# A hybrid decoder trunk on one core: the DeltaNet inverse issued in one piece, with z projections, weight subtractions and output heads moved around it

## The chip, the cores and the metric

The kernel runs on one core of a Trainium2 chip, in float32 throughout. TensorE (PE) multiplies in a float32 form that the kernel makes exact enough by splitting each operand into a high and a low part: each product of two split operands is three matmuls. VectorE (DVE), ScalarE (ACT) and GpSimd (POOL) work beside it, and DMAs for the weights are issued from SyncE's queue (SP). The metric is the device time of one execution in microseconds; the median of several runs is compared. A difference is judged against the spread of these runs.

## The reference

Two layers over a sequence of 256 tokens, width 1024. Each layer adds half a SwiGLU, a mixer and another half SwiGLU, each on an RMS-normalised input; a final RMS norm follows. The mixer of layer 0 is a gated DeltaNet, that of layer 1 a sliding-window attention with sinks. What the change touches is the DeltaNet mixer:

```python
def mixer_gated_deltanet(h, w_in, w_conv, A_log, dt_bias, out_norm, w_out):
    proj = h @ w_in                                  # q, k, v (8 heads x 128 each), z, b, a
    qkv = jax.nn.silu(causal_depthwise_conv(qkv, w_conv))          # 4 taps
    q = l2norm(q) * 128 ** -0.5;  k = l2norm(k)
    beta = sigmoid(b);  g = -exp(A_log) * softplus(a + dt_bias)
    o = gated_delta_rule_chunked(q, k, v, g, beta)   # chunks of 64 tokens
    o = rmsnorm(o, out_norm) * jax.nn.silu(z)
    return o @ w_out
```

Inside the delta rule a unit lower triangular system (I + L) sol = rhs is solved for every head and chunk, with L from k, beta and the decay; sol gives u and w, and a scan over the chunks carries the state S. The kernel solves it by forming the inverse of I + L from small blocks upwards.

## The kernel before, in words

The input is 2 tiles of 128 tokens (t = 0, 1). Weights come in pieces of 128x1024: `split` (L287) issues a DMA into `raw` (4 buffers), ACT casts it to `whi` (L307), and an engine, DVE unless POOL is named, subtracts to get `wlo` (L308). `whi` and `wlo` have 5 buffers each. `wcols` (L319) fetches a chunk of 256 columns as two such pieces; `npool` says how many of them POOL subtracts. PSUM has four slots psA (projections) and four psB (everything else).

The order of instructions on each engine is set ahead of time: the kernel is traced in program order, which is the priority, and a planner lists the instructions by estimated readiness. `issue_after(ins)` puts the instructions of a block behind `ins` on that engine's queue. `Ticker` interleaves by hand: generators are added, and each `tick()` runs every one of them to its next `yield`.

The DeltaNet mixer (`gdn`, L672) runs as follows.

- Two chunks of z (`zproj`, L926) for both tiles, with the gates `gdn_gates` as a generator beside them. The gates end in four Exps into `Dt` (L666); `res["exp"]` is the last of them that is traced so far. A third chunk of z follows (`zmore`, L961).
- Four k chunks by `conv` (L908): two tiles of 24 matmuls each into `pcv`, a copy scaled by the fourth tap on ACT (L915, tile `cv`, pool c1 with 5 buffers), the three other taps on DVE (L918), and a Silu on ACT (L922) issued after `res["exp"]`. Behind each chunk a generator `kpost` transposes (L705), sums squares (L712), forms k k^T (L730) times the decay into `nf` (L731), and after every second chunk `blocks` cuts out the diagonal blocks and masks them on POOL (L759, L761).
- Behind the last k chunk the generator `inverse` (L766 on) inverts the 16x16 diagonal blocks of all heads on DVE, in three pieces with a `yield` between them, and starts two generators `chain`, which build the 128x128 inverses from the blocks by small matmuls on PE (L824, L844, L856, L864, L872, L878).
- Four v chunks and four q chunks by the same `conv`; `vpost` and `qpost` follow them. `state` carries the scan; `first` computes the outputs of heads 0 to 3 for t = 0 ahead of the end of the q chunks. The fourth chunk of z comes behind the third q chunk. `zgate` applies Silu to z on ACT and multiplies the output norm into it on POOL (L935).
- The end: w_out in 8 rows of 128 (`out_weights`, rows 3 and 4 subtracted on POOL), the outputs of the heads (`o_of`), their norm (`post`, L1042 to L1050), a transpose to the output's layout (`turn`, L1057 to L1061) and the output projection into `acc`, then `after(t)`, the norm for the next FFN.

The attention mixer (`swa`) fetches its w_out by the same `out_weights`, with rows 4 and 6 subtracted on POOL.

Of the kernel before, what the change touches and what calls it, by code (L numbers as in the profile page):

```python
# [24 lines left out]
H = 8  # L25
# [188 lines left out]
class Kern:  # L214
# [72 lines left out]
    def split(self, src, hi, lo, shape, eng=None, cuts=1):  # L287
        nc = self.nc
        raw = self.wp.tile(shape, F32, tag="raw", name="raw", bufs=4)
        n = shape[1] // cuts  # L290
        parts = [slice(i * n, (i + 1) * n) for i in range(cuts)]
        if len(src.shape) == 4:
            for k in range(shape[1]):
                nc.sync.dma_start(out=raw[:, k].rearrange("p (g f) -> p g f", g=2), in_=src[:, k])
        else:
            nc.sync.dma_start(out=raw, in_=src)
        with ExitStack() as behind:
            if self.hold is not None:
                self.hold[0] -= 1
                if self.hold[0] < 0:  # L300
                    for ins in self.hold[2:]:
                        behind.enter_context(self.tc.issue_after(ins.ins))
                self.hold[1] -= 1
                if not self.hold[1]:
                    self.hold = None
            for c in parts:
                nc.scalar.copy(hi[:, c], raw[:, c])  # L307
                (eng or nc.vector).tensor_tensor(out=lo[:, c], in0=raw[:, c], in1=hi[:, c].bitcast(F32), op=ALU.subtract)  # L308

    def wpiece(self, src, a, b, eng=None, pool=None):  # L310
# [5 lines left out]
        self.split(src, hi, lo, [P, a, b], eng)  # L316
        return hi, lo
# [20 lines left out]
    def wrow(self, w, k, pool=None, eng=None):  # L338
        hi, lo = self.wpiece(w[k * P:(k + 1) * P, :].unsqueeze(1), 1, D, eng=eng, pool=pool)
        return hi[:, 0, :], lo[:, 0, :]  # L340

    def wrow2(self, w, k, eng):
        hi = self.big([P, 2, 1, D], "whi2", F32R)
        lo = self.big([P, 2, 1, D], "wlo2", F32R)
        out = []
        for i in range(2):
            self.split(w[(k + i) * P:(k + i + 1) * P, :].unsqueeze(1), hi[:, i], lo[:, i], [P, 1, D], eng(k + i))
            out.append((hi[:, i, 0, :], lo[:, i, 0, :]))
        return out
# [216 lines left out]
    def gdn_prep(self, w_in, w_conv, A_log, dt_bias, out_norm):  # L566
# [13 lines left out]
        onb = self.row_bc(out_norm, P, "onb")  # L580
        wcr = self.small([96, P], "wcr", 1)
        nc.scalar.dma_start(out=wcr, in_=w_conv.rearrange("j (t c) -> (j t) c", c=P))
        return wh, wl, expA, dtb, onb, wcr
# [88 lines left out]
    def gdn(self, nrm, prep, w_in, w_out, after):  # L672
        nc = self.nc
        M = self.M
        wabh, wabl, expA, dtb, onb, wcr = prep
# [90 lines left out]
        def inverse():  # L766
# [21 lines left out]
            yield  # L788
# [13 lines left out]
            yield  # L802
# [6 lines left out]
            nc.vector.transpose(yx[:, 1].rearrange("p u c -> p (u c)"), yx[:, 0].rearrange("p u c -> p (u c)"))  # L809
# [98 lines left out]
        def conv(col0, dst, npool, start):  # L908
            w = self.wcols(w_in, col0, npool)
            for f in range(2):  # L910
# [5 lines left out]
                for j in (2, 1, 0):  # L916
                    s = 3 - j
                    nc.vector.scalar_tensor_tensor(  # L918
                        out=c[:, s:], in0=ps[:, 0:T - s], scalar=wc[:, j, ct:ct + 1],
                        in1=c[:, s:], op0=ALU.mult, op1=ALU.add)  # L920
# [11 lines left out]
        def zgate(t, hs, keep=lambda ins: ins):  # L932
            z = zs[:, t, hs]
            keep(nc.scalar.activation(z, z, AF.Silu))
            keep(nc.gpsimd.tensor_tensor(  # L935
                out=z, in0=z, in1=onb.unsqueeze(1).to_broadcast([P, hs.stop - hs.start, P]), op=ALU.mult))

        def zgates():
            n = 2 * zc[0]
            for t in range(NT):  # L940
                yield
                zgate(t, slice(0, n), self.tc.keep_in_program_order)
# [16 lines left out]
        zc = [2]  # L959

        def zmore(n):  # L961
            for c in range(zc[0], zc[0] + n):
                w = self.wcols(w_in, 3 * D + c * 256)
                for t in range(NT):
                    zproj(c, t, w)
                    tk.tick()
            zc[0] += n
# [36 lines left out]
        def state():  # L1004
# [16 lines left out]
            for g in range(2):  # L1021
                pw = four("pws", lambda o, i: mm(o, wT[:, 4 * g + i, :], S[:, 4 * g + i, :]))
                for i in range(4):
                    h = 4 * g + i
                    nc.vector.scalar_tensor_tensor(out=u[:, 1, h, :], in0=pw[:, i, :], scalar=nbr[:, 1, h:h + 1],
                                                   in1=u[:, 1, h, :], op0=ALU.mult, op1=ALU.add)
            yield
# [10 lines left out]
        def post(t, g):  # L1038
# [10 lines left out]
            for i in range(4):  # L1049
                nc.vector.scalar_tensor_tensor(out=on[:, i, :], in0=po[t, g][:, i, :], scalar=f[:, i:i + 1],  # L1050
                                               in1=zs[:, t, 4 * g + i, :], op0=ALU.mult, op1=ALU.mult)
            ons[t, g] = on

# [9 lines left out]
        def first():  # L1063
            o_of(0, 0)
            post(0, 0)
            yield
            yield
            turn(0, 0)
            yield
# [3 lines left out]
        for c in range(4):  # L1073
            conv(c * 256, lambda f: late["qT"][:, 2 * c + f, :], 1, [qpost(c)])
            if c == 0:
                tk.add(state())
            if c == 1:
                tk.add(then(first))
            if c == 2:
                n = 2 * zc[0]  # L1080
                w = self.wcols(w_in, 3 * D + 3 * 256)
                for t in range(NT):
                    zproj(3, t, w)
                    zgate(t, slice(n, H))
                    tk.tick()
# [3 lines left out]
        o_of(0, 1)  # L1089
        post(0, 1)  # L1090
        o_of(1, 0)
        acc = [self.psA("acc") for n in range(2)]
        for n in range(2):
            self.out_part(acc[n], ob[0], ws, n, range(0, 4))
        turn(0, 1)
        post(1, 0)
        o_of(1, 1)
        turn(1, 0)
        for n in range(2):
            self.out_part(acc[n], ob[0], ws, n, range(4, KT))  # L1100
            self.out_add(acc[n], 0, n)
        post(1, 1)
        turn(1, 1)
        after(0)
        for n in range(2):
            a = self.psA("acc")
            self.out_part(a, ob[1], ws, n, range(KT))
            self.out_add(a, 1, n)
# [30 lines left out]
    def swa(self, nrm, prep, w_in, w_out, after):  # L1139
# [112 lines left out]
        ws = self.out_weights(w_out, (4, 6))  # L1252
# [113 lines left out]
```

## Time and profile before

| what | before |
|---|---|
| median of 3 runs | 1028.65 us (1027.06 to 1029.8) |
| profiled execution, its own time | 1026.73 us |
| its span | 1025.0 us |
| mean granted TensorE clock | 0.996 |
| subtractions of weights in the DeltaNet stage | 31 on DVE, 12 on POOL |
| the same in the attention stage (740 to 840 us) | 21 on DVE, 2 on POOL |

In rows of the timeline the columns are the start in us, the duration in us, the engine, the line, the operation with tiles and shapes, the count, and in brackets the idle time before it with what released it. In rows of busy time by stretches the columns are the stretch, its length, then for each engine that worked (in the order PE, weight loads, DVE, ACT, POOL) the busy time with the number of instructions, and at the end the granted clock, the DMA share and GB/s; a row asked for one line has only the engines of that line. In rows of groups the busy time and the mean in ns follow the bar.

### The profile page before, as it was taken

To read this page: it belongs to the slowest core of one execution; us is meant where nothing else is said; L and a number is where in the kernel's file an instruction comes from. 1 tells how busy PE (TensorE), PEld (TensorE's weight loads), DVE (VectorE), ACT (ScalarE), POOL (GpSimd) and SP (SyncE) were. 2 spreads that over 40 slices of the span, in tenths; PEclk is the share of its full clock that TensorE was granted. 3 is DMA by queue.
4 is the path that set the end of the run, shared out by engine and by line. 5 is a ranking of instruction groups with operands and counts; after the bars stand their busy time and mean duration, and the time that the engine had idled before them with its cause. 6 is when DMAs were issued, how large, how long until landed. Compare 5 with 4: busy or idle time off the path is not lost.

```text
span 1025.0 us, 16468 instructions
## 1 busy us (share of the span) xinstructions
PE 999.7 (98%) x6195; PEld 871.3 (85%) x6195; DVE 648.1 (63%) x971; ACT 550.8 (54%) x1007; POOL 232.6 (23%) x269
## 2 busy tenths in 40 slices
PE   8999999999979899999999999999999999999997
PEld 7888888899878888888888888888898678888886
DVE  6865654666896666666546666664568756666544
ACT  6755544457755645555534555553366645555442
POOL 0124510016753201332200122230021301323100
PEclk9999999999989999999999999999999999999999
DMA  7766665644443335666665666666653436666651
GB/s 248 238 185 169 198 208 182 203 150 127 134 128 104 103 103 179 192 189 186 200 196 178 196 191 190 185 206 195 196 191 118 128 99 208 201 187 185 203 187 42
DMA packets 135316, 177.05 MB, mean 173 GB/s; under 512 B 7250, under 2 KB 120260, under 8 KB 135236
## 3 DMA queue, kind: packets, MB, share of 16 engines
q1 hardware_dynamic: 132032, 171.46, 54.6%
q10 hardware_dynamic: 3204, 4.53, 1.4%
q8 instruction: 49, 0.80, 0.3%
q14 instruction: 31, 0.25, 0.1%
HBM read 174.92 MB, written 1.05 MB: 172 GB/s over the span
## 4 chain that ended last, share of the span: by engine, by line
PE 62%; issue 1%; DVE 1%; ACT 1%; DMA 0%; POOLq 0%; POOL 0%; SPq 0%; DVEq 0%; ACTq 0%
PE pg L361 11%; PE pu L361 11%; PE acc L356 7%; PE acc L354 7%; PE acc L355 7%; PE pu L362 6%; PE pg L362 6%; PE pgu L356 1%; PE pgu L355 1%; PE pgu L354 1%; PE pq L354 1%; PE pq L356 1%; PE pq L355 1%; PE psc L1190 1%; PE po L1234 1%
## 5 line engine op out<-in xcount | busy, mean ns | idle before, releaser
L308 DVE TENSOR_TENSOR wlo<-raw,whi 128x1024 fp32r<-128x1024 f32 (+1 forms) x304 | 378.2, 1247 | 202.6 <-ACT whi L307 200.9
L307 ACT CAST whi<-raw 128x1024 fp32r<-128x1024 f32 (+1 forms) x318 | 330.1, 1046 | 186.7 <-PE acc L356 82.7
L361 PE MATMUL pg<-hs,whi 128*128 128x512 f32 x624 | 219.5, 394 | 0.0
L361 PE MATMUL pu<-hs,whi 128*128 128x512 f32 x624 | 219.4, 393 | 0.0
L362 PE MATMUL pu<-hs,wlo 128*128 128x256 f32 x624 | 175.5, 281 | 0.0
L362 PE MATMUL pg<-hs,wlo 128*128 128x256 f32 x624 | 174.6, 281 | 0.0
L361 PEld LDWEIGHTS pg<-hs,whi 128*128 128x128 f32 x624 | 117.0, 188 | 26.0
L469 POOL TENSOR_TENSOR act<-act,gate 128x256 f32<-128x256 f32 x78 | 58.6, 751 | 354.7 <-DVE act L468 345.9
L361 PEld LDWEIGHTS pu<-hs,whi 128*128 128x128 f32 x624 | 117.0, 187 | 25.9
L355 PE MATMUL acc<-wlo,ah 128*128 128x512 f32 (+1 forms) x340 | 128.5, 378 | 0.0
L356 PE MATMUL acc<-whi,al 128*128 128x512 f32 (+1 forms) x340 | 128.4, 378 | 0.0
L354 PE MATMUL acc<-whi,ah 128*128 128x512 f32 (+1 forms) x340 | 128.0, 378 | 0.0
L362 PEld LDWEIGHTS pg<-hs,wlo 128*128 128x128 f32 x624 | 118.2, 189 | 0.4
L362 PEld LDWEIGHTS pu<-hs,wlo 128*128 128x128 f32 x624 | 118.2, 189 | 0.0
L354 PEld LDWEIGHTS acc<-whi,ah 128*128 128x128 f32 x340 | 64.1, 188 | 12.1
L355 PEld LDWEIGHTS acc<-wlo,ah 128*128 128x128 f32 x340 | 64.1, 188 | 11.7
L356 PEld LDWEIGHTS acc<-whi,al 128*128 128x128 f32 x340 | 64.0, 188 | 11.8
L472 POOL TENSOR_SCALAR ah<-act 128x256 fp32r<-128x256 f32 x78 | 66.4, 851 | 6.7
L354 PE MATMUL pcv<-hs,whi 128*128 128x256 f32 x192 | 56.5, 294 | 5.9 <-DVE cv L918 5.9
L458 ACT COPY gate<-pg 128x256 f32<-128x256 f32 x78 | 28.7, 368 | 52.6 <-PE pg L362 52.6
L467 ACT COPY act<-pu 128x256 f32<-128x256 f32 x78 | 28.7, 368 | 52.0 <-PE pu L362 52.0
L356 PE MATMUL pcv<-hs,wlo 128*128 128x256 f32 x192 | 55.9, 291 | 0.0
(340 smaller groups left out, 1522.8 us busy)
## 6 DMA issues: line engine op xcount, KB each, us to landing
raw<-in_ffn_w_gu_dram SPq DMA_DIRECT2D x156, 512.0 KB, 4.5
raw<-in_ffn_w_down_dram SPq DMA_DIRECT2D x88, 512.0 KB, 4.2
raw<-in_a_w_in_dram SPq DMA_DIRECT2D x32, 512.0 KB, 4.1
raw<-in_ffn_w_gu_dram SPq DMA_DIRECT2D x40, 256.0 KB, 4.8
raw<-in_b_w_in_dram SPq DMA_DIRECT2D x12, 512.0 KB, 4.8
raw<-in_a_w_out_dram SPq DMA_DIRECT2D x8, 512.0 KB, 4.3
raw<-in_b_w_out_dram SPq DMA_DIRECT2D x8, 512.0 KB, 3.6
nw<-in_ffn_norm_dram ACTq DMA_DIRECT2D x3, 512.0 KB, 4.2
```

Source lines behind the costliest of these rows:

```text
L307: nc.scalar.copy(hi[:, c], raw[:, c])
L308: (eng or nc.vector).tensor_tensor(out=lo[:, c], in0=raw[:, c], in1=hi[:, c].bitcast(F32), op=ALU.subtract)
L354: nc.tensor.matmul(out, lhsT=lh, rhs=rh, start=start, stop=False)
L355: nc.tensor.matmul(out, lhsT=lh, rhs=rl, start=False, stop=False)
L356: return nc.tensor.matmul(out, lhsT=ll, rhs=rh, start=False, stop=stop)
L361: nc.tensor.matmul(out, lhsT=lh, rhs=r2, start=start, stop=False)
L362: return nc.tensor.matmul(out[:, :T], lhsT=ll, rhs=rh, start=False, stop=stop)
L458: nc.scalar.copy(g, pg[:, T:])
L467: nc.scalar.copy(a, pu[:, T:])
L469: nc.gpsimd.tensor_tensor(out=a, in0=a, in1=gates[f], op=ALU.mult)
L472: ahead[2] = nc.gpsimd.tensor_scalar(oh, a, 1.0, None, op0=ALU.mult)
L1190: nc.tensor.matmul(out, lhsT=qT[:, j, b * P:(b + 1) * P], rhs=kz[:, kv, :, kt * P:(kt + 1) * P], start=True, stop=True)
```

## The change

- `inverse` loses its two `yield`s, so all its steps are traced at once, and its last transpose is kept as `late["inv"]`.
- `conv` loses `npool`, and takes `behind`: the three taps on DVE of v chunks 0 and 1 are issued after `late["inv"]`. `self.hold = [0, 2, late["inv"]]` ahead of v chunk 2 does the same with the subtractions of its two weight pieces.
- z chunk 2 moves from ahead of the k convolutions to behind them; z chunk 3 moves there from the q convolutions.
- No weight subtraction is left on POOL, neither in the convolutions nor for w_out of either mixer.
- The output norm is no longer multiplied into z on POOL; it scales the rows of w_out as they are cast (ACT) and subtracted (DVE, now multiply and subtract in one instruction). It is loaded as one column.
- `heads(g)` replaces `first`: once the state is complete, the outputs of heads 0 to 3 are computed for both tiles during the q convolutions. At the end only heads 4 to 7 are left, w_out comes in two halves (the second half's subtractions behind the first `post` of the end), and the output projection has four accumulators open at a time.

```diff
@@ split
+            if rows is not None:
+                nc.scalar.activation(hi, raw, AF.Copy, scale=rows)
+                nc.vector.scalar_tensor_tensor(out=lo, in0=raw, scalar=rows, in1=hi.bitcast(F32),
+                                               op0=ALU.mult, op1=ALU.subtract)
+                return
@@ out_weights
-    def out_weights(self, w_out, pooled):
-        eng = lambda k: self.nc.gpsimd if k in pooled else None
-        ws = [self.wrow(w_out, k, eng=eng(k)) for k in range(4)]
-        return ws + self.wrow2(w_out, 4, eng) + self.wrow2(w_out, 6, eng)
+    def out_weights(self, w_out, half, rows=None):
+        if half == 0:
+            return [self.wrow(w_out, k, rows=rows) for k in range(4)]
+        return self.wrow2(w_out, 4, rows) + self.wrow2(w_out, 6, rows)
@@ inverse
-            yield
             for h in (4, 8):
...
-            yield
...
-            nc.vector.transpose(yx[:, 1]..., yx[:, 0]...)
+            late["inv"] = nc.vector.transpose(yx[:, 1]..., yx[:, 0]...)
@@ conv
-        def conv(col0, dst, npool, start):
-            w = self.wcols(w_in, col0, npool)
+        def conv(col0, dst, start, behind=None):
+            w = self.wcols(w_in, col0)
...
+                with ExitStack() as later:
+                    if behind is not None:
+                        later.enter_context(self.tc.issue_after(behind.ins))
+                    for j in (2, 1, 0):
+                        ...
@@ order of the stage
-        zmore(1)
         for c in range(4):
...
-            conv(D + c * 256, lambda f: kT[:, 2 * c + f, :], c // 2, [then(*steps)])
+            conv(D + c * 256, lambda f: kT[:, 2 * c + f, :], [then(*steps)])
             if c == 3:
                 tk.tick()
+        zmore(2)
+        zmore(3)
         for c in range(4):
             vT = self.c2([P, 2, T], "vT")
-            conv(2 * D + c * 256, lambda f: vT[:, f, :], 1, [vpost(c, vT)])
+            if c == 2:
+                self.hold = [0, 2, late["inv"]]
+            conv(2 * D + c * 256, lambda f: vT[:, f, :], [vpost(c, vT)], late["inv"] if c < 2 else None)
@@ heads
-        def first():
-            o_of(0, 0)
-            post(0, 0)
...
+        def heads(g):
+            while "state" not in late:
+                yield
+            for t in range(NT):
+                o_of(t, g)
+                post(t, g)
+                yield
+            for t in range(NT):
+                yield
+                turn(t, g)
...
             if c == 1:
-                tk.add(then(first))
-            if c == 2:
-                ... z chunk 3 ...
+                tk.add(heads(0))
         tk.drain()
-        ws = self.out_weights(w_out, (3, 4))
+        ws = self.out_weights(w_out, 0, onc)
...
+        for t in range(NT):
+            o_of(t, 1)
+            on = post(t, 1)
+            if not t:
+                self.hold = [0, 4, on]
+                ws += self.out_weights(w_out, 1, onc)
+        for n in range(2):
+            out(0, range(0, 4), n)
+        turn(0, 1)
+        for n in range(2):
+            out(0, range(4, KT), n)
+            self.out_add(acc[0][n], 0, n)
+        for n in range(2):
+            out(1, range(0, 4), n)
+        turn(1, 1)
+        after(0)
+        for n in range(2):
+            out(1, range(4, KT), n)
+            self.out_add(acc[1][n], 1, n)
@@ attention mixer
-        ws = self.out_weights(w_out, (4, 6))
+        ws = self.out_weights(w_out, 0) + self.out_weights(w_out, 1)
```

More of the change, by code (lines that the diff above doesn't have):

```diff
@@ L808, in inverse @@
                                     op=ALU.mult)
-            nc.vector.transpose(yx[:, 1].rearrange("p u c -> p (u c)"), yx[:, 0].rearrange("p u c -> p (u c)"))
+            late["inv"] = nc.vector.transpose(yx[:, 1].rearrange("p u c -> p (u c)"),
+                                              yx[:, 0].rearrange("p u c -> p (u c)"))
             late["yx"] = yx
@@ L958, in gdn, with zmore @@
             tk.tick()
[L959 to L967, printed above, removed]
-        zmore(1)
+        def zmore(c):
+            w = self.wcols(w_in, 3 * D + c * 256)
+            for t in range(NT):
+                zproj(c, t, w)
+                tk.tick()
         for c in range(4):
@@ L1073, in gdn @@
         for c in range(4):
[L1074 removed]
+            conv(c * 256, lambda f: late["qT"][:, 2 * c + f, :], [qpost(c)])
             if c == 0:
```

72 lines of the change are left out of this document (24 added, 48 removed).

## The prediction

> **What bounds the kernel now.** I read the page's first part, then the busy time by stretches, then PE's own waits in the timeline, then DVE, POOL and ACT around them.
>
> ```profile
> span 1025.0 us, 16468 instructions
> PE 999.7 (98%) x6195; PEld 871.3 (85%) x6195; DVE 648.1 (63%) x971; ACT 550.8 (54%) x1007; POOL 232.6 (23%) x269
> ```
>
> PE is the bound, with 25 us idle in all. The change touches the DeltaNet mixer (and the output weights of the attention mixer), so its ceiling is PE's idle time there. By stretches (PE busy is the second number):
>
> ```profile
> 218.45:376.88 158.43, 145.64 (x1466) 136.07 (x1465) 119.95 (x235) 97.55 (x258) 68.60 (x51) 0.98 0.39 121
> 270.00:280.00 10.00, 8.57 (x72) 8.37 (x71) 9.80 (x20) 4.40 (x11) 4.71 (x3) 1.00 0.53 163
> 280.00:290.00 10.00, 7.00 (x59) 6.80 (x57) 10.00 (x16) 5.57 (x9) 6.50 (x3) 0.97 0.36 105
> 290.00:300.00 10.00, 7.14 (x47) 7.17 (x48) 10.00 (x19) 3.88 (x7) 0.95 (x1) 0.69 0.48 157
> 350.00:360.00 10.00, 6.67 (x45) 5.64 (x45) 4.98 (x15) 6.11 (x27) 2.01 (x2) 1.00 0.61 196
> ```
>
> From the first k convolution (218.45) to the next FFN's first matmul (376.88) PE is busy 145.64 of 158.43 us: 12.79 idle. DVE stands at 9.8 to 10 of 10 from 270 to 300, and there PE waits; the granted clock falls to 0.69. The waits themselves:
>
> ```profile
> 273.01 0.44 PE L705 MATMUL pvn<-ident,vT 128*128 128x128 f32 x2 [1.43 <-ACT vT L922]
> 292.86 0.55 PE L354 MATMUL pcv<-hs,whi 128*128 128x256 f32 x1 [5.86 <-DVE cv L918]
> 294.28 0.42 PE L354 MATMUL pcv<-hs,whi 128*128 128x256 f32 x1
> 296.18 0.28 PE L354 MATMUL pcv<-hs,whi 128*128 128x256 f32 x1
> 311.49 0.69 PE L844 MATMUL pt<-X,nf 32*32 32x32 f32 x32 [1.20 <-DVE X L835]
> 355.56 0.30 PE L1057 MATMUL poT<-ident,on 128*128 128x128 f32 x1 [2.71 <-DVE on L1050]
> ```
>
> The long one, 5.86 us, is PE out of PSUM slots while conv taps queue among the steps of the inverse. Behind it matmuls take 0.42 instead of 0.28 us until 296.18: 3.3 us at about half rate, 1.65 lost. So 12.79 + 1.65 = 14.4 us is the most that this stage can give, and 144.0 us of PE work lies in it.
>
> **The change, part by part.**
>
> **z chunk 2 moves from ahead of the k convolutions to behind them, z chunk 3 from the q convolutions to the same place.** The work is equal, only its place changes:
>
> ```profile
> 196.72:202.47 5.75, 5.75 (x48) 5.71 (x47) 0.37 (x1) 1.00 0.84 256
> 228.00:242.00 14.00, 4.09 (x8) 1.23 (x8) 1.00 0.49 149
> 247.10 0.60 PE L705 MATMUL pkn<-ident,kT 128*128 128x128 f32 x4
> 248.35 0.36 PE L355 MATMUL pcv<-hs,whi 128*128 128x256 f32 x1
> ```
>
> A chunk of 48 matmuls is 5.75 us of PE, two weight transfers on SP's queue, two casts on ACT and two subtractions on DVE; all of these move with it and their number stays. The k convolutions then begin at 218.45 - 5.75 = 212.7, and 144.0 + 5.75 = 149.75 us of PE work follow. PE can do without the inverse: the gates' row sums 4.1 (second row), four k chunks 23.0, their transposes and products 4 x 1.25 (247.10 to 248.35) = 5.0, two z chunks 11.5, and the first two v chunks 11.5, in all 55.1. It runs out at 212.7 + 55.1 = 267.8: the v taps of these two chunks now wait for the inverse, and their four tiles hold all four psA slots. What is left behind the inverse is 149.75 - 55.1 = 94.6 us.
>
> **When does the inverse end?** Its beginning:
>
> ```profile
> 233.38 2.37 POOL L308 TENSOR_TENSOR wlo<-raw,whi 128x1024 fp32r<-128x1024 f32 x1
> 224.16 2.30 DVE L632 TENSOR_TENSOR gr<-gr,gs 128x16 f32<-128x16 f32 x1
> 243.95 1.28 ACT L922 ACT_TABLE_LOAD   x1
> 245.25 1.64 ACT L922 ACTIVATE kT<-cv 128x256 f32<-128x256 f32 x5
> 267.54 2.40 POOL L308 TENSOR_TENSOR wlo<-raw,whi 128x1024 fp32r<-128x1024 f32 x1
> 267.65 3.37 DVE L308 TENSOR_TENSOR wlo<-raw,whi 128x1024 fp32r<-128x1024 f32 x1 [0.55 <-PE pcv L356]
> 270.94 2.42 DVE L918 SCALAR_TENSOR_TENSOR cv<-pcv,wc,cv 128x255 f32<-128x255 f32 x5
> 273.28 1.08 DVE L771 STREAM_TRANSPOSE tw<-d 128x512 f32<-128x512 f32 x1
> ```
>
> The k convs' Silus wait for the decay's last Exp, which ends at 243.95; the inverse starts 28 us after the first Silu. Ahead of the Exp, without POOL's subtractions, go 2.4 us between the third and fourth mask product (233.38) and 2.1 us in which a 16-element DVE product stood still (224.16, 2.30 us long). Against this stands a new cost: with two z ticks fewer ahead of the k convs, the first k tile's Silu is issued after the Exps of t = 0 and ahead of those of t = 1, so ACT changes tables twice more, 2 x 1.28 = 2.6. Net 4.5 - 2.6 = 1.9 us earlier (bounds -2, if the earlier taps also slow the gates' chain, and 4.5). The Trainium skill, "ScalarE: Activation LUTs", What ACT_TABLE_LOAD costs, puts a switch at about 2.66 us, with a drain behind the load; here the first Silu stands 0.02 us behind the load's end, so the trace disagrees, and by the page the time would be about 2.8 us more than I forecast. Between Silu and inverse go POOL's subtraction that stands in front of the masks (267.54, 2.4), the five v taps ahead of the first transpose (2.42; they are now behind it), and one lock wait of a subtraction ahead of the products nf, about 1.0 (bounds 0 and 2.1, what 267.65 shows: 3.37 against 1.23 plain). Sum: 273.28 - 1.9 - 2.4 - 2.4 - 1.0 = 265.6 (bounds 262 to 270).
>
> ```profile
> 273.28:298.20 24.92, 7.61 (x18) 0.86 0.52 164
> 273.28:298.20 24.92, 5.87 (x4) 0.86 0.52 164
> L799 DVE TENSOR_TENSOR tw<-iw,inv 128x64 f32<-128x64 f32 x2 | 2.5, 1306 | 0.0
> L774 DVE TENSOR_TENSOR inv<-tw 128x256 f32<-128x256 f32 x1 | 2.0, 2029 | 0.0
> L796 DVE TENSOR_TENSOR tw<-inv 128x64 f32<-128x64 f32 x2 | 0.4, 264 | 0.0
> ```
>
> The inverse took 24.92 us, of which 7.61 were conv taps (18, first row) and 5.87 subtractions of weights (4, second row): 11.44 by itself. POOL's lock is in that (L799 has the size of L796: 2.5 against 0.4; L774 lost some 1.6), 3.7 us; but its steps overlapped with the fillers, which alone they can't. I take 11.0 (bounds 7.7 and 14). The end: 276.6 instead of 298.2.
>
> **The wait that comes with it.** Queued behind the inverse on DVE are the 12 taps of v chunks 0 and 1 (12 x 0.42 = 5.0, from 7.61 / 18), and both subtractions for v chunk 2, without which PE can't go on.
>
> ```profile
> 300.22 1.31 PE L824 MATMUL pt<-yx,d 32*32 32x32 f32 x128
> 810.50 1.23 DVE L308 TENSOR_TENSOR wlo<-raw,whi 128x1024 fp32r<-128x1024 f32 x1
> ```
>
> PE waits 276.6 - 267.8 = 8.8 us, then has the chains' block products (1.31 the first pair, as much the second) and v's transposes, about 4, while DVE needs 5.0 + 1.23 = 6.2 before the next conv: 2.2 more. Bounds 0.5 (taps and subtractions interleaved) and 6 (chain steps ahead of them).
>
> **No GpSimd subtractions.** Twelve here go to DVE: 14.8 us more DVE work at 1.23.
>
> ```profile
> 190.00:380.00 190.00, 44.02 (x31) 29.58 (x12) 0.98 0.40 123
> ```
>
> DVE's 31 took 44.02 us, 1.42 each against 1.23 plain, so about 6 us of lock waits in these alone, and 6 more in the rows above go. DVE's total stays about equal; I count nothing beyond the terms above. If that cover fails (DVE full from 276 to 320), it is in the upper bound of the wait. Folding the output norm into w_out's rows replaces four POOL products by a scale on the same eight casts and subtractions: nothing, hidden behind convs.
>
> **Half of the heads early.** The 2.71 us wait for the normalised heads at 355.56 is to go: group 0's outputs give PE 48 matmuls that need no group 1. I leave 0.3 us at the tail (bounds 0 and 2.7; the 8 subtractions for w_out, 9.8 us of DVE, are what would be late next).
>
> **Attention mixer.** Its two POOL subtractions go to DVE.
>
> ```profile
> 804.41 5.73 POOL L308 TENSOR_TENSOR wlo<-raw,whi 128x1024 fp32r<-128x1024 f32 x2
> 805.51 2.38 DVE L308 TENSOR_TENSOR wlo<-raw,whi 128x1024 fp32r<-128x1024 f32 x1
> 808.14 2.02 DVE L1206 SCALAR_TENSOR_TENSOR smx<-smx,sk 128x4 f32<-128x4 f32 x1
> 812.12 0.73 PE L356 MATMUL acc<-whi,oTl 128*128 128x512 f32 x2 [1.65 <-DVE oTl L1239]
> ```
>
> Lock waits of 1.15 and 1.87 us go, 2 x 1.23 of work come: 0.6 of the 1.65 us wait (bounds -1 and 1.65).
>
> **The sum.** PE waits after the change 8.8 + 2.2 + 0.3 = 11.3 against 14.4: 3.1 gained; with 0.6, 3.7 us; I round to 4 for the small waits of 0.2 to 0.6 that I did not count. The profiled execution took 1026.73 us (1.7 outside its span), 1.9 below the median 1028.65 of the runs. 1026.73 - 4 = 1022.7 by the profiled one, 1024.6 against the median.
>
> **The rivals.** *The cover suffices:* ACT, relieved of v's casts and Silus, brings the masks at 262, and the inverse alone takes 8 to 9: it ends at 271, PE waits 3 + 1.5. Gain 10, time 1019. For it: all lock waits gone. Against: ACT, not DVE, paces the 28 us from Silu to inverse.
>
> *It only moves the wait:* the gates' chain gains nothing, the inverse ends at 279, PE waits 11.2 + 2.5: no change, 1028. For it: the chain from gates to Exp doesn't hang on z, and PE could formerly run ahead through all of v and half of q, now only through half of v.
>
> *Slower:* the wait at v chunk 2. If the inverse ends at 281 and DVE does the 12 taps, the chains' steps and then the subtraction, PE waits 13.2 + 6: 4.8 more than now, 1033.5. It decides once both waits pass 14.4 + 3.
>
> *Clock:* the wait of 8.8 us is longer than the 5.86 that halved the clock, and PE restarts on block products. If the half rate lasts through these 4 us and 3.3 us of convs, as it lasted behind 292.86, 2.0 + 1.65 come on top: 1028. The Trainium skill, "TensorE: Matmul & The Clock Gate", What's actually happening, has the full clock back only after about 3.4 us of sustained work; the 3.3 us of slow matmuls here agree.
>
> **How the numbers follow.** Changes within 0.3% (3.1 us) are about what a measurement of this kernel can't tell from none. Chances: forecast 0.35, cover 0.22, moved 0.20, clock 0.08, slower 0.15. Of the forecast's own range (1021 to 1028) three quarters are faster: 0.26 + 0.22 = 0.48 faster; 0.09 + 0.20 + 0.05 = 0.34 same; the rest, 0.18, slower. The range takes the cover case at its lower end and the slower one short of its full price: 1017.5 to 1032.
>
> **What would show it.** Right: one PE wait of 7 to 11 us near 268 released by a v tap or v subtraction; inverse steps without L918 rows between, ending near 276.6; no POOL rows of L308; two more table loads between 235 and 245; no wait above 1 us at the transposes of the last heads. Wrong: an inverse that ends before 271 or after 280, or a second wait above 4 us between 277 and 330, where DVE would be full.

## The result, and the profile after

The changed kernel takes 1041.74 us (1041.29 to 1042.0) against 1027.93 us (four runs of the kernel before; the prediction had three of them, with a median of 1028.65): 1.0136 of the time before, with a 95% interval of 1.0122 to 1.015. The forecast was 1024.6 us, in a range of 1017.5 to 1032. The profiled execution is 1041.29 us long, 14.6 us more than the one of before; its span is 14.6 us longer too.

Busy time by stretches, from the first matmul of z to the first of the next FFN, and from there to the end, first of before, then of the changed kernel (behind the length stands PE's busy time):

```profile
196.72:376.88 180.16, 167.14 (x1643) 157.17 (x1642) 131.61 (x255) 109.02 (x278) 69.16 (x52) 0.98 0.40 123
376.88:1025.00 648.12, 638.84 (x3556) 549.45 (x3554) 394.77 (x555) 333.74 (x564) 121.36 (x142) 1.00 0.58 177
```

```profile
194.63:389.39 194.76, 171.90 (x1644) 161.46 (x1642) 131.24 (x265) 110.60 (x276) 32.36 (x36) 0.93 0.37 113
389.39:1039.58 650.19, 639.52 (x3555) 549.99 (x3555) 397.06 (x559) 335.90 (x567) 115.21 (x140) 1.00 0.59 177
```

The stage is 14.6 us longer (194.76 - 180.16), and it holds the same matmuls. PE's idle time in it went from 13.0 to 22.9 us (length less busy), 9.8 more; and the same matmuls fill 4.8 us more (171.90 - 167.14) because the clock is 0.93 in place of 0.98. I call the second part stretch. The rest of the program is 2.1 us longer, and z begins 2.1 us earlier. The second is scatter: in the profiles of all versions here z begins between 194.63 and 197.02 us.

The timeline of PE in the changed kernel, the rows with an idle time of 0.6 us or more in this stage and one matmul of the conv behind the inverse:

```profile
243.43 0.35 PE L359 MATMUL pz<-whi,hs 128*128 128x256 f32 x1 [1.81 <-DVE cv L926]
279.77 1.93 PE L829 MATMUL pt<-yx,d 32*32 32x32 f32 x128 [9.64 <-DVE yx L813]
283.58 1.39 PE L829 MATMUL py<-yx,t 32*32 32x32 f32 x87 [1.35 <-issue]
289.13 0.58 PE L359 MATMUL pcv<-hs,whi 128*128 128x256 f32 x1 [4.15 <-DVE cv L926]
289.94 0.41 PE L359 MATMUL pcv<-hs,whi 128*128 128x256 f32 x1
352.29 0.94 PE L897 MATMUL pkq<-qT,kT 128*128 128x128 f32 x6 [0.78 <-ACT qT L930]
355.24 0.50 PE L359 MATMUL acc<-whi,oT 128*128 128x512 f32 x1 [1.01 <-ACT oT L1062]
370.72 0.50 PE L359 MATMUL acc<-whi,oT 128*128 128x512 f32 x1 [0.67 <-ACT oT L1062]
375.13 0.80 PE L359 MATMUL acc<-whi,oT 128*128 128x512 f32 x1 [2.78 <-ACT oT L1062]
```

One wait for the inverse of 9.64 us is followed by a second of 4.15 us for a conv tap. Where the clock was low:

```profile
240.00:250.00 10.00, 8.19 (x57) 8.03 (x57) 2.34 (x6) 9.91 (x23) 1.27 (x2) 0.83 0.17 54
270.00:280.00 10.00, 0.36 (x19) 0.26 (x21) 9.50 (x26) 0.47 (x1) 1.67 (x2) 0.77 0.00 0
280.00:290.00 10.00, 4.50 (x259) 4.23 (x252) 9.80 (x16) 2.31 (x5) 0.00 (x0) 0.50 0.63 202
370.00:380.00 10.00, 6.55 (x21) 4.98 (x21) 7.88 (x12) 4.21 (x5) 0.00 (x0) 0.72 0.84 251
```

In the trace's clock records the half rate lasts 3.41, 17.07 and 6.83 us in this stage, 27.3 in all; before it was one stretch of 6.83 us. DVE's timeline shows the inverse without a tap in it (its first and last row) and what was put behind it:

```profile
269.16 1.09 DVE L777 STREAM_TRANSPOSE tw<-d 128x512 f32<-128x512 f32 x1 [2.55 <-POOL d L767]
...
278.91 0.71 DVE L813 STREAM_TRANSPOSE yx<-yx 128x512 f32<-128x512 f32 x1
279.55 1.61 DVE L926 SCALAR_TENSOR_TENSOR cv<-pcv,wc,cv 128x255 f32<-128x255 f32 x4
281.08 4.62 DVE L313 TENSOR_TENSOR wlo<-raw,whi 128x1024 fp32r<-128x1024 f32 x4
285.61 1.65 DVE L926 SCALAR_TENSOR_TENSOR cv<-pcv,wc,cv 128x254 f32<-128x254 f32 x4
287.46 1.23 DVE L313 TENSOR_TENSOR wlo<-raw,whi 128x1024 fp32r<-128x1024 f32 x1 [0.20 <-ACT whi L312]
288.60 0.47 DVE L926 SCALAR_TENSOR_TENSOR cv<-pcv,wc,cv 128x253 f32<-128x253 f32 x1
```

Five weight subtractions (5.85 us) stand between the taps of the four held-back tiles, so no PSUM slot comes free until the third tap of the first tile ends at 289.1.

### The profile page after: what moved, and what is told of

Its sections match the earlier page's. It is cut to its first block, busy times and chain, and to the rows that moved or that the text cites. A ratio compares the mean times of both kernels' runs of the same rounds, so it can differ in the third digit from the quotient of the medians.

```text
span 1039.6 us, 16450 instructions
## 1 busy us (share of the span) xinstructions
PE 1002.9 (96%) x6195; PEld 875.7 (84%) x6195; DVE 650.2 (63%) x985; ACT 555.3 (53%) x1007; POOL 189.8 (18%) x251
## 4 chain that ended last, share of the span: by engine, by line
PE 87%; ACT 5%; DVE 3%; issue 2%; DMA 1%; POOL 1%; SPq 0%; POOLq 0%; ACTq 0%; DVEq 0%
PE pg L366 14%; PE pu L366 14%; PE acc L359 9%; PE acc L360 8%; PE acc L361 8%; PE pu L367 7%; PE pg L367 7%; PE pgu L361 2%; PE pgu L360 2%; PE pgu L359 2%; PE pcv L359 2%; PE pcv L360 2%; PE pcv L361 2%; ACT whi L312 1%; PE pq L359 1%
## 5 line engine op out<-in xcount | busy, mean ns | idle before, releaser
L312 ACT CAST whi<-raw 128x1024 fp32r<-128x1024 f32 (+1 forms) x310 | 322.5, 1046 | 190.8 <-PE acc L361 82.1
```

## The experiments

Each time is the median; the ratio is to the kernel before on the same chip, with its 95% interval. The intervals reach 1 to 4 us to either side; where those of two versions overlap, the times alone do not show a difference between them.

| version | us | ratio to before |
|---|---|---|
| changed kernel | 1041.74 | 1.0136 (1.0122 to 1.015) |
| decay Exps first | 1041.59 | 1.0132 (1.01 to 1.0164) |
| taps free | 1040.29 | 1.0113 (1.0073 to 1.0152) |
| old end | 1041.91 | 1.0139 (1.0107 to 1.0171) |
| attention on GpSimd | 1039.57 | 1.0113 (1.0086 to 1.014) |
| convs on GpSimd | 1042.04 | 1.0125 (1.0089 to 1.016) |
| z and taps as before | 1033.51 | 1.0049 (1.0029 to 1.007) |
| before, DVE subtracts | 1026.97 | 0.9988 (0.9966 to 1.0011) |
| before, inverse in one go | 1026.42 | 0.9978 (0.9958 to 0.9997) |
| both of these | 1026.51 | 0.9984 (0.9972 to 0.9996) |
| before, z late | 1033.78 | 1.0062 (1.0037 to 1.0086) |
| before, heads early | 1033.04 | 1.0046 (1.0023 to 1.0069) |
| taps free, unread matmuls | 1035.01 | 1.0068 (1.0041 to 1.0095) |
| changed, unread matmuls | 1039.16 | 1.0119 (1.0088 to 1.015) |
| both, two unread per step | 1022.84 | 0.9949 (0.9933 to 0.9965) |
| both, one unread per step | 1021.38 | 0.9936 (0.9919 to 0.9954) |
| both, z in the chain | 1025.31 | 0.9976 (0.9963 to 0.9988) |

**Undoing one part of the changed kernel.** Two ticks more ahead of the k convs, so that all decay Exps come first:

```diff
+        for _ in range(2):
+            tk.tick()
         for c in range(4):
             steps = [lambda c=c: kpost(c)]
```

> The changed kernel with one edit: all four decay Exps are issued before the first Silu of the k convs, so that two of the ACT table loads that the change added (1.28 us each) go away and the gate chain is not behind a Silu any more. Theory A (PE waits for the inverse, then for taps that are queued behind it): the inverse starts about 2 to 3 us earlier, the 1.81 us wait of PE at the z chunk goes, and the time is 1036 to 1039 us, some 3 to 5 below the changed kernel's 1041.7; the 4.15 us wait behind the inverse stays. Rival B (the added table loads are the main cause): 1033 or below, and PE's wait at the inverse shrinks under 5 us. Rival (DVE's sum is the bound of the stage, where it waits does not matter): within 1 us of 1041.7.

Nothing is won that can be measured. The number of the third expectation holds (1041.59), but not its reason, since DVE is busy only 131.19 of 193.11 us of the stage; the other two miss. The wait for the inverse fell from 9.64 to 6.7 us, but PE now waits 4.22 us for the first k tiles to come out of ACT:

```profile
195.46:388.57 193.11, 170.71 (x1644) 160.72 (x1642) 131.19 (x265) 108.53 (x274) 32.09 (x36) 0.94 0.36 114
```

PE's idle time in the stage is 22.4 us, about as much as with the loads (22.9). A wait moved from the inverse's end to its front.

Taps of v chunks 0 and 1 not held back:

```diff
-            if c == 2:
-                self.hold = [0, 2, late["inv"]]
-            conv(..., [vpost(c, vT)], late["inv"] if c < 2 else None)
+            conv(..., [vpost(c, vT)])
```

> The changed kernel with one edit: the taps of the first two v chunks are not held back behind the inverse, so they may be placed before it or wherever a gap is; the inverse is still issued in one go, and z, the heads and the subtractions stay as changed. Theory A: PE has two v chunks to do while the inverse runs, its 9.64 us wait shrinks to a few us and the 4.15 us wait behind the inverse goes with the half clock that follows them; 8 to 10 us are won, near 1032 to 1034 us. Rival (DVE's sum is the bound): the taps only delay the inverse by their 6 to 7 us, the wait is the same in another place and the time stays within 2 us of 1041.7.

The waits did what theory A said, and the time did not: it stays in the rival's range, without the rival's reason. The four executions spread from 1035.05 us (mean clock 0.987) to 1042.23 (0.979), and the profile is of the slowest. Idle time in the stage fell from 22.9 to 14.2 us, but the stretch ate it. The stage of this version, then the time from 301.61 to 335.74, all at half rate:

```profile
196.47:389.44 192.97, 178.76 (x1643) 168.09 (x1642) 129.90 (x265) 111.12 (x276) 33.59 (x36) 0.90 0.38 114
301.61:335.74 34.13, 29.80 (x520) 0.51 0.09 29
```

The busy time grew by 6.9 us for the same matmuls. PE was 29.8 of 34.1 us busy there, and still the clock did not come back. The reason to suspect is in what PE ran: all dense v convs were done, and beside the chain's 32x32 and 64x64 products stood only runs of at most twelve dense ones, at 0.41 us each:

```profile
314.79 2.19 PE L869 MATMUL px<-ident,yf 64*64 64x64 f32 x16
316.91 1.11 PE L711 MATMUL pvn<-ident,vT 128*128 128x128 f32 x4
317.96 1.97 PE L877 MATMUL pt<-xa,nf 64*64 64x64 f32 x16
...
320.23 0.41 PE L360 MATMUL pcv<-hs,whi 128*128 128x256 f32 x1
```

The old end of the mixer (`first`, two accumulators, w_out in one piece; its diff is the change's "heads" part reversed):

> The changed kernel with one edit: the end of the mixer is as before, with no half of the heads done early and the last four heads' halves split as before; the inverse, z and the subtractions on DVE stay as changed. Theory C (the new end costs its own 0.67 + 2.78 us of waits and the half clock behind them): 4 to 5 us are won, near 1037 us, and the accumulators' waits are 3.3 us in all as before the change. Rival (the waits come from the subtractions that DVE now has in the end of the stage, not from the order of the heads): under 2 us won, and the waits of the accumulators stay at 3 us or more with DVE behind its subtractions.

Nothing is won, as the rival has it. A 4.07 us wait for the normalised heads is back, up to 368.34. The rival's reason is not what ended it: DVE is through its last three output-weight subtractions at 360.1, has idle time behind them, and just ahead of the norm waits for ACT's sums of squares (`junk`):

```profile
355.94 4.15 DVE L308 SCALAR_TENSOR_TENSOR wlo<-raw,onc,whi 128x1024 fp32r<-128x1024 f32 x3
365.98 0.16 DVE L1045 SCALAR_TENSOR_TENSOR fo<-ssq,so 128x4 f32<-128x4 f32 x1 [2.46 <-ACT junk L1043]
```

The attention mixer's two subtractions on GpSimd again:

```diff
-        ws = self.out_weights(w_out, 0) + self.out_weights(w_out, 1)
+        ws = [self.wrow(w_out, k) for k in range(4)] + self.wrow2(w_out, 4, None, pool) + self.wrow2(w_out, 6, None, pool)
```

> The changed kernel with one edit: in the attention mixer GpSimd again does its two subtractions of the output weights, and DVE is freed of them. Theory D: the attention stage's waits fall from 3.9 us to about 2.2 and its half clock goes, and 2 us are won, near 1039.7 us; the stages ahead of it stay the same to 0.3 us. Rival (those waits are a matter of a transfer or of ACT): no change within 0.5 us.

Theory D holds on size: 2.2 us won by the medians, and the waits there are those of before again. The waits in the attention stage, first of the changed kernel, then with this edit:

```profile
829.96 0.44 PE L1236 MATMUL po<-att,v 128*64 128x128 f32 x4 [1.22 <-ACT att L1228]
832.13 1.13 PE L1236 MATMUL po<-att,v 128*64 128x128 f32 x8 [1.73 <-DVE att L1229]
```

```profile
824.69 0.73 PE L361 MATMUL acc<-whi,oTl 128*128 128x512 f32 x2 [1.65 <-DVE oTl L1241]
829.96 0.44 PE L1236 MATMUL po<-att,v 128*64 128x128 f32 x4 [0.23 <-DVE oTl L1241]
```

A part of the 2.2 us is chance. From the first matmul of the next FFN to the end the changed kernel takes 650.19 us and this version 647.22. All ten profiles with GpSimd's two subtractions lie between 647.22 and 648.63. Of the eight with all on DVE five lie between 648.64 and 648.90; the three others, the changed kernel among them, lie between 650.19 and 651.06, and in these the clock falls to half for 3.41 us near 832. So the move costs about 1 us, and some 2 us more where the clock falls.

Ten conv subtractions on GpSimd again (`npool=1` for v and q, `c // 2` for k):

> The changed kernel with one edit: GpSimd again does one subtraction in two of the weights of the k convs 2 and 3, all v convs and all q convs (10 subtractions); the output weights stay on VectorE. Theory (the moved subtractions stand between the held-back taps and are most of the loss): the 4.15 us wait behind the inverse shrinks below 1.5 us, and 4 to 8 us are won, 1034 to 1038 us. Rival (the single stretch of inverse without dense work beside it is the loss): the 9.64 us wait stays and under 2 us are won; GpSimd may even lengthen the inverse.

By the time the rival holds: no gain, and the wait for the tap is still 3.5 us. The wait for the inverse fell to 6.12 us, but 3.65 us of waits for Silus at the k transposes (0.67 and 2.98) came. Behind the inverse only two DVE subtractions stand between the taps here, yet they take 5.49 us, 2.7 each beside two of GpSimd's (5.63 us), against 1.23 plain. Giving subtractions back to GpSimd does not win back the loss in the convs.

**One part alone on the kernel before.** DVE subtracts everything in the DeltaNet stage:

```diff
-            conv(..., c // 2, ...)   # k;  1 for v and q
+            conv(..., 0, ...)
-        ws = self.out_weights(w_out, (3, 4))
+        ws = self.out_weights(w_out, ())
```

> The kernel before with one edit: in the DeltaNet stage all weight subtractions are VectorE's, none GpSimd's (12 subtractions of 1.2 us each move; the attention stage keeps GpSimd's two). Theory (these fill VectorE where it was already busy 10.0 of 10 us, from 280 to 300 us, and this is most of the change's loss): 4 to 9 us slower, 1031 to 1036 us, with TensorE's wait for the taps at the v convs grown from 5.86 us and more half clock. Rival (VectorE's other instructions become shorter once GpSimd is quiet, since VectorE's whole busy time rose only 2.1 us with the change): within 2 us of before.

The rival holds: no difference that can be measured. DVE's busy time in the stage rises only from 131.61 to 132.49 us with twelve subtractions more. The 5.86 us wait is gone and idle time in the stage fell from 13.0 to 9.8 us; the clock took 1.9 us of that back (PE busy 169.03 us, against 167.14), with 13.7 us at half rate behind the inverse.

The inverse in one go (its two `yield`s removed):

> The kernel before with one edit: the inverse is issued in one go, without the two places where it let the planner put other work between its parts; nothing is held back behind it. Theory (one go costs: the taps stand behind 10 us of inverse, and TensorE waits): 2 to 6 us slower. Rival (one go ends the inverse earlier, and the small products get dense matmuls of the v convs beside them): 1 to 3 us faster, with the 5.86 us wait smaller. Third: the planner places the instructions by its own costs, and the order hardly changes: within 1 us.

The rival fits best: 2.3 us faster by the ratio (interval 0.3 to 4.3), and the 5.86 us wait is down to 3.29. Together:

> The kernel before with the two parts that alone cost nothing (0.9988 and 0.9978 of before): VectorE does all weight subtractions of the DeltaNet stage, and the inverse is issued in one go. If they add up: 1023 to 1026 us, 0.997 of before or less. If each only shifts TensorE's wait at the v convs to the chain behind the inverse: 1026 to 1030 us, no change.

Both gains together would give 0.9966; the ratio is 0.9984, in the range of no change, though the intervals of the two parts do not rule out that they add up. This is the telling profile. PE's idle time in the stage is 7.5 us, against 13.0 before, and the time hardly moves, since 23.9 us behind the inverse run at half rate:

```profile
195.16:376.11 180.95, 173.48 (x1644) 163.44 (x1642) 131.92 (x267) 110.81 (x278) 41.52 (x40) 0.93 0.40 122
```

Chunks 2 and 3 of z behind the k convs:

```diff
-        zmore(1)                     # chunk 2, ahead of the k convs
         for c in range(4):           # k convs
...
+        zmore(2)                     # chunks 2 and 3
-            if c == 2:               # q convs
-                ... zproj(3, t, w); zgate(...) ...
```

> The kernel before with one edit: the third and fourth chunk of z both stand behind the k convs (before: the third ahead of them, the fourth among the q convs). Theory (the fourth chunk was the dense work that TensorE had beside the chain of small products and the state, and the move also puts two table loads among the k convs): 5 to 12 us slower, 1033 to 1040 us, with more half clock behind the inverse than the 6.83 us of before. Rival (as predicted: the k convs start earlier, so the inverse does, and time is won): 1020 to 1027 us.

Half of the heads early, with the new end:

> The kernel before with one edit: half of the heads done early and the new order at the end of the mixer, with the output weights unscaled and rows 3 and 4 still subtracted by GpSimd; z, k, v and the inverse as before. Theory (the new end costs its two waits for the last heads and a half clock): 2 to 6 us slower. Rival (the end's waits come from what stands ahead of it, as the old end in the changed kernel won nothing): within 1.5 us of before.

Each costs alone, by the ratios: 6.4 us (0.62%) and 4.7 us (0.46%). The stage rows of the two:

```profile
195.42:383.83 188.41, 173.05 (x1643) 162.61 (x1642) 130.36 (x254) 112.03 (x276) 67.33 (x50) 0.95 0.37 117
196.85:384.81 187.96, 172.75 (x1643) 160.51 (x1641) 128.84 (x253) 106.95 (x276) 69.18 (x52) 0.95 0.38 117
```

Both have some 2 us more idle time (15.4 and 15.2 against 13.0) and 5.6 to 5.9 us of stretch. With z late the half clock is not where the theory put it: 3.41 us of it lie behind the inverse (6.83 before), and 17.1 us in four places of the stage. The 5.86 us wait is gone, but 3.6 us of waits for Silus at the k transposes are new, and the wait for the normalised heads at the end grew from 2.71 to 4.06 us.

Reversed in the changed kernel, z and the held-back taps together:

> The changed kernel with two edits: z as before (third chunk ahead of the k convs, fourth among the q convs) and no taps held back; the inverse in one go, no GpSimd subtractions and the heads stay as changed. If z and the held-back taps are the loss: 1025 to 1031 us, at the level of before, with the half clock behind the inverse under 14 us. If the heads and the new end are the loss: 1034 us or more, and the kernel before with the heads alone loses as much.

It fell between the two expectations: 8.2 us are won, and 5 us above before are left, about the heads (4.7) and the attention stage (2.2) less what the two harmless parts give (1.6). The half clock behind the inverse is not under 14 us but 23.9, as in the kernel before with these two parts.

**The clock by itself.** Matmuls whose result nobody reads, 128x256 by the identity, in PE's waits. In the version with free taps ten ahead of the inverse's end, then two behind each of the chain's first four steps:

```diff
+        def keep(n):
+            ps = self.psB("keep")
+            for _ in range(n):
+                nc.tensor.matmul(ps[:, 0:256], lhsT=self.ident, rhs=late["keep"][:, 0:256], start=True, stop=True)
...
             nc.scalar.copy(t32, blockwise(self.psB("pt1"), off, X0))
+            keep(2)
             yield
```

> The run with the free taps, plus TensorE matmuls whose result nobody reads: ten in front of the first small product of the inverse (there TensorE waited 3.89 us), and two behind each of the first four steps of each half of the chain of small products. They add some 11 us of TensorE work, most of it in its waits. Theory (the half clock is what ate the gain of the free taps: 34.13 us at half rate, and in its own four runs 1035.05 us at a mean clock of 0.987 against 1042.23 at 0.979, about 0.43 us for each us of half rate): the half rate behind the inverse falls to 10 us or less and the time to 1028 to 1034 us. Rival (the half clock only fills time in which the chain of small products waits for ACT and DVE in any case): the time stays at 1039 to 1043 us or rises, with a clock near 0.99.

```profile
301.61:335.74 34.13, 33.60 (x620) 1.00 0.16 48
```

The same 34.13 us run at full clock, and 5.3 us are won by the medians though 26 matmuls are added, 1 us short of the theory's range. The runs of the two versions overlap (1035.05 to 1042.23 and 1033.17 to 1038.04 us), so this pair alone does not settle it; the pair further down, with one unread matmul per step, does.

> The changed kernel plus TensorE matmuls whose result nobody reads: twenty in its 9.64 us wait for the inverse, and ten between the first four small products, in front of the 4.15 us wait. They price the half clock of this stretch alone, since the waits stay. If the clock's cost is what its matmuls show (3.4 us of dense matmuls at half rate behind the wait, some 5 us of small products): the 17.07 us of half rate go and 2.5 to 4 us are won, 1038 to 1039.5 us. If the waits are all that counts: 1041 to 1043 us.

2.6 us by the medians, as priced, but not clear of noise: the intervals overlap, and one of the four runs took 1044.39 us. In its profile 3.41 us of half rate are left in the stage, and those at z and at the end are gone too, so 2.6 us is no price of the long wait alone.

> The version with VectorE's subtractions and the inverse in one go (1026.5 us, 7.3 us of waits in the stage, but 23.9 us of half rate behind the inverse), plus two unread matmuls behind each of the first four steps of each half of the chain, some 7 us of TensorE work. If a half clock of 24 us costs 0.43 us each and the added work is half in waits: 1017 to 1022 us. If it is bound by the chain's length: 1026 to 1032 us.

1022.84 us, 0.8 above the first range, and no half rate is left in the stage.

> The same with one unread matmul behind each of these steps, some 3.5 us of TensorE work. If one is enough to keep the clock: 1016 to 1020 us, below the version with two. If the clock needs more: half rate stays above 14 us and the time is 1023 to 1029 us.

One unread matmul behind each of eight steps is enough: 1021.38 us, 0.9936 (0.9919 to 0.9954) of before, the lowest median here, 1.4 us above the range, and 5.1 us below the same kernel without them; the intervals of these two do not overlap. Its stage:

```profile
195.30:372.31 177.01, 171.26 (x1659) 159.07 (x1658) 131.42 (x267) 110.81 (x278) 41.49 (x40) 0.99 0.41 125
```

PE is busy 2.2 us less with eight matmuls more, and its idle time fell from 7.5 to 5.8 us. Up to the inverse's end both run in step: the first block product starts at 304.42 us without and at 304.50 with them. So the half clock was a cause of the lost gain. The stretches of 3.41 us behind the inverse's end, without and with them (length, PE's busy time, clock, DMA share, GB/s):

```profile
305.21:308.62 3.41, 1.66 (x103) 0.96 0.54 159
308.62:312.03 3.41, 1.65 (x102) 0.50 0.02 6
312.03:315.44 3.41, 2.03 (x64) 0.50 0.00 0
315.44:318.85 3.41, 3.41 (x77) 0.50 0.02 5
318.85:322.26 3.41, 3.41 (x28) 0.50 0.02 5
322.26:325.67 3.41, 3.41 (x38) 0.50 0.00 0
325.67:329.08 3.41, 3.41 (x27) 0.50 0.00 0
329.08:332.49 3.41, 3.41 (x19) 0.54 0.02 5
332.49:335.90 3.41, 3.41 (x33) 1.00 0.00 0
```

```profile
305.21:308.62 3.41, 1.58 (x71) 1.00 0.55 162
308.62:312.03 3.41, 3.41 (x72) 0.50 0.02 5
312.03:315.44 3.41, 3.00 (x102) 1.00 0.02 5
```

The clock fell in both; with one unread matmul in each step it was back after one stretch, without them after seven.

Real work in their place, the fourth chunk of z tied behind the chain's first products:

```diff
+                    with self.tc.issue_after(late["small"].ins):
-                    zproj(3, t, w)
+                        zproj(3, t, w)
```

> The version with VectorE's subtractions and the inverse in one go, with no unread matmuls: the fourth chunk of z (5.8 us of dense work) may start only behind the first products of the chain, where it stood in front of the inverse's end. If dense work beside the chain keeps the clock and TensorE finds other work ahead of the inverse's end: half rate under 10 us and 1016 to 1023 us. If TensorE then waits those 5.8 us for the inverse: the wait at the first small product grows from 0.43 us to 5 or 6 us, the clock falls there instead, and the time is 1025 to 1031 us.

The second expectation came true, with a longer wait than it had: PE waits 9.4 us for the inverse, the clock falls there, and the half rate ends after 13.7 us, while the dense z runs. At 1025.31 us it is 3.9 us slower than letting z go ahead and burning eight matmuls.

## Why the prediction was wrong, point by point

- **The ceiling** of 14.4 us follows from its rows, and the change lost as much as there was to gain (14.6). The time lies above every rival too; the slower one ended at 1033.5. One of the prediction's signs of being wrong came: a second wait above 4 us behind the inverse, 4.15, with DVE full. The forecast's own sum, by spans: 1022.7 - 1.7 = 1021.0 forecast, 1039.6 measured, 18.6 apart.
- **The sum** set all of PE's idle and slowed time before (14.4 us) against three named waits after (11.3). On the side of before, the waits and the slow stretch that it named are 5.86 + 2.71 + 1.65 = 10.2. So the gain of 3.1 rested on 4.2 us of other waits, 1.43 and 1.20 among them, that it put at nothing without a reason. New ones came in their place, at z and at the end.
- **k convs earlier, PE dry at 267.8, inverse from 265.6 to 276.6, PE's wait 8.8:** right in kind. PE ran dry at 270.1, the inverse ran from 269.16 to 279.62, 10.5 us long, and PE waited 9.64. The gates' chain came out just past its worse bound (-2): one Silu went ahead, but the row of five that the inverse hangs on started 2.1 us later (247.36 against 245.25), not 1.9 earlier; with the two table loads taken out again, nothing was won that can be measured.
- **The wait at the second v chunk, 2.2 (bounds 0.5 to 6):** mis-sized; 1.35 + 4.15 = 5.5. The order that it took for the good case, taps and subtractions interleaved (0.5), is the one that came: 5.85 us of subtractions stand between the taps, and no tile is through its third tap before them. No run changed this order alone.
- **What I left out at the front:** 1.81 us at z behind the k convs. A z chunk waits there for a PSUM slot that a tap on DVE has to free, and the tap waits for its copy on ACT, which is busy 9.91 of 10 us there (DVE 2.34); I moved z and asked for no wait in its new place.
- **The tail, 0.3 (bounds 0 to 2.7):** wrong, 0.78 + 1.01 + 0.67 + 2.78 + 0.29 = 5.5 us. The wait for the normalised heads went and one for their transposed output came. The sentence that named the output weights' subtractions as "late next" named what stands there (2 x 2.47 us of them around 368 to 374), without a price. The longest wait, 2.78 us up to 375.13, is for a copy that stands on ACT behind a cast of the next FFN's weights, and this cast waits for its transfer:

```profile
373.54 1.05 ACT L312 CAST whi<-raw 128x1024 fp32r<-128x1024 f32 x1 [2.88 <-DMA raw<-in_ffn_w_gu_dram]
374.49 0.58 ACT L1062 CAST oT<-poT 128x512 fp32r<-128x512 f32 x1
```

The chain that ended last leads there from the normalised heads over a held-back subtraction (368.40) and the transfer (from 370.27, 3.19 us). That holding the subtractions back made the transfer late is read from this chain; no run tried it.

- **The clock:** this is the step that failed most. The sum took it that no half rate is left and put it at nothing; it was a rival with a chance of 0.08 and 3.65 us for one place. Against that premise the stretch is 1.65 + 4.8 = 6.4 us, and it came in three places. That a half clock costs time is shown by the unread matmuls in the version with both harmless parts (5.1 us); in the changed kernel itself their 2.6 us are not clear of noise.
- **The attention mixer, 0.6 gained (bounds -1 to 1.65):** wrong in sign; 2.1 us lost in this profile, 2.2 won back by undoing it. About 1 us of it is in all profiles, within the bound; the rest came with the clock. Freeing DVE from the lock wait did not pay for two more subtractions: the chain that ended last runs there through two of DVE's (825.52, 1.56 us, and 829.67, 1.80 us), between the steps of the softmax.
- **GpSimd's subtractions:** right. DVE's busy time went from 648.1 to 650.2 us with 14 subtractions more, and doing this alone in the DeltaNet stage changed nothing that can be measured.

The misses add up: waits 11.4 (22.7 for 11.3), clock 6.4, attention 2.7, less 2.1 for z's earlier start, which is scatter, 18.4 of 18.6.

By parts, z and the heads by their ratios and the rest by medians: DVE subtractions and the one-go inverse -1.6, z late 6.4, heads 4.7, held-back taps 1.5 (1041.74 less 1040.29), attention 2.2, in all 13.2 of the 13.8 us measured. That this comes so near is partly luck: each part has an interval of 1 to 4 us, the taps' 1.5 us is not clear of noise, and the folded output norm was not tried alone. Nor is the sum a law: the heads cost 4.7 us on the kernel before, and undone in the changed one they gave nothing. In both versions with z late and the old end, PE waits 4.06 and 4.07 us for the normalised heads, against 2.71 before. That z's chunk had been the filler there is argued from the profiles; only its cost is shown.

## What to carry over

A wait removed from a busy engine is worth its length only if what stands there instead keeps the clock: read the stage's idle time and its busy time side by side, and a version whose waits shrink while its busy time grows has paid in clock. Before moving dense work, ask which stretch of small dependent products it was filling, in the place it leaves as well as where it goes. Price each part of a composite change alone: here two parts were free, two cost 6.4 and 4.7 us, two more 1 to 2 us near the noise, and the two free ones together had cut the idle time from 13.0 to 7.5 us and lost it again to the clock.

## What was not expected of the hardware

The length of a wait does not tell how long the half clock lasts; what runs behind it matters more. A 9.64 us wait with dense convs behind it cost 17.07 us of half rate. In the version with both harmless parts no wait around it was over 1.75 us, and the half rate lasted 23.9 us, with PE busy 3.41 of 3.41 us in four stretches in a row. The Trainium skill, "TensorE: Matmul & The Clock Gate", What's actually happening, gives the full clock back after one busy window of about 3.4 us. The lengths here agree with the window, all multiples of 3.41; read with the profile's busy time, in which the ends of matmuls are modelled, the rule does not hold, since small products count as busy there and did not lift the clock. One unread 128x256 matmul behind each step, 0.70 us long at full clock, did. But in the version with free taps twelve conv matmuls in a row (from 319.85 to 322.77) did not. What the gate counts is not shown.
